# Down-projection: raw blocks in idle FFN slots by turns, second-half features stored split, gate weights split beside the last product

## The chip, the cores and the metric
The kernel runs on one core of a Trainium2 chip. Its engines are TensorE (PE, matmuls; PEld is its weight load), VectorE (DVE), ScalarE (ACT), GpSimd (POOL) and SyncE (SP), which here only issues DMAs. The metric is the time of one execution on the device in microseconds, median of several.

## The reference, cut to what matters
One decoder block in float32 on 1024 tokens of width 1024: two kinds of attention, an output projection, a gated MLP of width 2816, and a gated embedding added at the end. The change lies in the last two:

```python
h = rms_norm(x, g_pre_ffn[i])
u = causal_depthwise_conv(h @ w_up[i], conv_w[i], conv_b[i])
gate, val = jnp.split(u, 2, axis=-1)
f = (jax.nn.gelu(gate, approximate=True) * val) @ w_down[i]
x = x + rms_norm(f, g_post_ffn[i])
e = p[i] @ w_ple[i]
g = jax.nn.sigmoid(rms_norm(x, g_ple_gate[i]) @ w_ple_gate[i] + b_ple_gate[i])
x = x + rms_norm(g * e, g_post_ple[i])
```

## The kernel before
Every float32 operand of a matmul is split into a high part of type float32r (a cast on ACT, line 101) and the rest (a subtraction on DVE, or POOL, line 102); a product is high x high + low x high + high x low. `split` does this.

*Up-projection loop* (lines 1222 to 1250). 22 chunks of 128 features. For each chunk PE computes five products of 12 matmuls of a Strassen-like scheme. POOL and ACT prepare their weights, DVE adds partial sums into `u[0]` (gate) and `u[1]` (value), ACT writes the first tap of the convolution to PSUM (`y`), DVE adds two more, ACT applies gelu, DVE multiplies, and POOL stores the 128x1024 features to `f_dram[c]`. The loop's tiles live in the pool `up`: `p1`, `q0`, `q1` (128x512), `u0`, `u1`, `f` (128x1024), two slots each; `wr` with six slots for raw weights, `s` with four for sums.

*Down-projection* (from line 1305). The features of chunks 0 to 10 (first half) and 11 to 21 (second half), tokens 0 to 511 and 512 to 1023, and the two column halves of `w_down` make a 2x2x2 scheme with seven products instead of eight. Each product has 11 steps, one for each pair of chunks; each step (`down`) loads raw blocks, forms sums or differences on DVE, splits both operands, and issues 12 matmuls into four PSUM banks. The functions `p1` to `p7` say which blocks a product takes: product 7 takes a 128x1024 row of features (`both`, tag `u0`) and two weight blocks (tags `q0`, `q1`); product 2 takes second-half features of tokens 0 to 511 and a weight block (both `wr`), product 4 the second-half features of tokens 512 to 1023 and a weight block. The products run as 1 with 5, then 6 with 3, then 7 with 2, then the rest of 7, then 4. Raw blocks come on SP's queue. The split features go to `s`, the split weights to `wh`, `wl` of the pool `stage`.

*End.* `finish` adds the residual to each finished row of tokens and transposes its norm; its steps are spread by `fill` over the last steps of products 7 and 4 and the gate stage. In the gate stage each of eight token tiles takes 48 matmuls with 16 weight blocks of `w_ple_gate` (8 for each column half), which `gate_weights` loads and splits while the first tile runs. The gain and bias rows (`b_ple_gate`, `g_post_ple`) are loaded after product 4, in a pool `gp` that takes the place of `up`.

The program text gives dependences and priorities; a scheduler sets the order of instructions on each engine when the kernel is built, and each engine and queue then works through its list in that order.

Of the kernel before, what the change touches and what calls it, by code (L numbers as in the profile page):

```python
# [9 lines left out]
F32 = mybir.dt.float32  # L10
# [8 lines left out]
P = 128  # L19
# [34 lines left out]
def tile_hybrid_block(ctx: ExitStack, tc: tile.TileContext, a: dict, out: bass.AP):  # L54
# [1168 lines left out]
    for c in range(NCH):  # L1223
# [22 lines left out]
        y = [conv(v, c, u[v]) for v in range(2)]  # L1246
        f = up_tile("f", S, 2)
        act.activation(f, y[0], AF.Gelu_apprx_tanh)
        dve.tensor_tensor(f, f, y[1], ALU.mult)
        pool.dma_start(f_dram[c], f)  # L1250
    y_cm.__exit__(None, None, None)
# [65 lines left out]

    def loaded(src, tag):
        t = up_tile(tag, 512, WR if tag == "wr" else 2)
        sp.dma_start(t, src)  # L1320
        return t

    def f_blk(i, th, k, tag):
        return loaded(f_dram[i + NP * k][:, halves_of[th]], tag)

    def w_blk(i, k, dh, tag):
        c = i + NP * k
        return loaded(a["w_down"][c * P:(c + 1) * P, halves_of[dh]], tag)

    def both(src):  # L1330
        t = up_tile("u0", S, 2)
        sp.dma_start(t, src)
        return t[:, :H], t[:, H:]

    def sub(dst, x, y):
        dve.tensor_tensor(dst, x, y, ALU.subtract)
        return dst

    b22 = {}

    def p1(i):
        return f_blk(i, 0, 0, "wr"), w_blk(i, 0, 0, "wr")

    def p5(i):
        a21, a22 = f_blk(i, 1, 0, "q0"), f_blk(i, 1, 1, "q1")
        b11, b12 = both(a["w_down"][i * P:(i + 1) * P, :])
        dve.tensor_tensor(store[0][i], a21, a22, ALU.add)
        return store[0][i], sub(store[1][i], b12, b11)

    def p6(i):  # L1350
        a11, b22[i] = f_blk(i, 0, 0, "q0"), w_blk(i, 1, 1, "p1")
        return sub(store[0][i], store[0][i], a11), sub(store[1][i], b22[i], store[1][i])

    def p3(i):
        a12 = f_blk(i, 0, 1, "q1")
        return sub(a12, a12, store[0][i]), b22.pop(i)

    def p7(i):
        a11, a21 = both(f_dram[i])
        b12, b22_ = w_blk(i, 0, 1, "q0"), w_blk(i, 1, 1, "q1")  # L1360
        return sub(a11, a11, a21), sub(b22_, b22_, b12)

    def p2(i):
        return f_blk(i, 0, 1, "wr"), w_blk(i, 1, 0, "wr")

    def p4(i):
        a22, b21 = f_blk(i, 1, 1, "wr"), w_blk(i, 1, 0, "wr")
        return a22, sub(b21, b21, store[1][i])

    def down(product, i, banks, fresh):  # L1370

        fr, w = product(i)
        wh, wl = [stage.tile([P, 512], F32R, tag=x, name=nm(x), bufs=4) for x in ("wh", "wl")]
        fh, fl = [up.tile([P, 512], F32R, tag="s", name=nm("f"), bufs=4) for _ in "hl"]
        split(fh, fl, fr)
        split(wh, wl, w)
        for t in range(4):
            tk = slice(t * P, t * P + P)
            for n, (l_, r_) in enumerate(((fh, wh), (fl, wh), (fh, wl))):
                pe.matmul(banks[t], l_[:, tk], r_, start=fresh and i == 0 and n == 0,  # L1380
                          stop=i == NP - 1 and n == 2, skip_group_check=not fresh)
# [68 lines left out]
    wg = {}  # L1450

    def gate_weights():
        for dh in range(2):
            for k in range(NK):
                src = a["w_ple_gate"][k * P:(k + 1) * P, dh * 512:dh * 512 + 512]
                if len(wg) < 4:
                    wg[dh, k] = split_w(src, 512, g_ple_gate[:, k:k + 1])
                else:
                    w = stage.tile([P, 512], F32, tag="ws", name=nm("ws"), bufs=3)
                    sp.dma_start(w, src)  # L1460
                    wh = gp.tile([P, 512], F32R, tag=f"gh{dh}{k}", name=nm("gh"))
                    wl = gp.tile([P, 512], F32R, tag=f"gl{dh}{k}", name=nm("gl"))
                    split(wh, wl, w, g_ple_gate[:, k:k + 1])
                    wg[dh, k] = (wh, wl)
                yield

    gw = gate_weights()
    for t in range(NT):
# [7 lines left out]
        for n, (c0, c1) in enumerate(zip(cuts, cuts[1:])):  # L1476
# [4 lines left out]
            for k in range(NK):  # L1481
                if t == 0:
                    next(gw)
# [80 lines left out]
```

## Time and profile before
| | us |
|---|---|
| median of three runs (lowest, highest) | 1541.58 (1540.2, 1546.6) |
| profiled execution | 1545.03 |
| its span, first to last instruction | 1543.3 |
| PE busy | 1400.3 |
| DVE busy | 1083.3 |
| ACT busy | 827.1 |
| POOL busy | 532.4 |

Windows in the text are microseconds from the start of the span. The up loop fills PE from about 907 to 1185; the down-projection's matmuls run from 1179 to 1418, product 7 with 2 from about 1320 to 1383 and product 4 to 1418; the gate stage follows. Matmul ends are modelled and overlap, so a busy PE is not a PE at its peak: what it should take is better counted in matmuls. Idle time in a group's row stands behind the second bar, with what ended it.

### The profile page before, as it was taken

The numbers are of one execution on the slowest core, as the hardware profiler recorded it, in microseconds if no ns is written. First come the engines' busy times: TensorE is split into PE (matmuls) and PEld (weight loads), VectorE is DVE, ScalarE is ACT, GpSimd is POOL, SyncE is SP. The second block draws the span as 40 slices with busy tenths as digits, with TensorE's granted clock in tenths as the row PEclk, the third lists the DMA queues.
The fourth block names the chain that finished last, engine by engine and source line by source line (L and its number), as shares of the span: only waits on it lengthen the run. The fifth ranks groups of instructions, "written<-read, shape, count | busy, mean of one in ns | idle before, by whom it ended". The sixth has DMA issues, their size and how long they took to land. (4 is left out here: it accounts for less than half of the span.)

```text
span 1543.3 us, 20396 instructions
## 1 busy us (share of the span) xinstructions
PE 1400.3 (91%) x6684; PEld 1146.5 (74%) x6684; DVE 1083.3 (70%) x1916; ACT 827.1 (54%) x1565; POOL 532.4 (34%) x567
## 2 busy tenths in 40 slices
PE   5998998988799898989998899999999999888995
PEld 3977786876578786767786678888887778666874
DVE  4569467799677867853447657666778876678897
ACT  6356465677677756654534444444444454345642
POOL 7106300003134335122232199989881000000233
PEclk9999999999899999999999899999999999999998
DMA  6031310104445525255648534444446963755554
GB/s 202 23 103 41 109 35 7 55 30 154 120 127 157 154 79 173 100 156 179 217 142 285 188 117 164 164 164 154 153 155 211 367 193 98 224 185 184 170 194 149
DMA packets 128779, 226.99 MB, mean 147 GB/s; under 512 B 13456, under 2 KB 50224, under 8 KB 128672
## 3 DMA queue, kind: packets, MB, share of 16 engines
q1 hardware_dynamic: 111488, 166.57, 34.2%
q0 software_dynamic: 17184, 59.11, 10.4%
q8 instruction: 53, 0.87, 0.2%
q14 instruction: 54, 0.44, 0.1%
HBM read 170.31 MB, written 55.31 MB: 146 GB/s over the span
## 5 line engine op out<-in xcount | busy, mean ns | idle before, releaser
L102 DVE TENSOR_TENSOR tl<-tr,th 128x512 fp32r<-128x512 f32 x192 | 103.2, 550 | 40.8 <-ACT th L101 34.7
L1217 DVE SCALAR_TENSOR_TENSOR y<-u,c_conv_w,y 128x1023 f32<-128x1023 f32 (+1 forms) x88 | 112.5, 1284 | 25.9 <-ACT y L1215 24.8
L101 ACT CAST th<-tr 128x512 fp32r<-128x512 f32 x192 | 91.1, 485 | 56.7 <-PE tr L468 45.0
L102 POOL TENSOR_TENSOR ws<-s,ws 128x512 fp32r<-128x512 f32 x84 | 109.7, 1313 | 15.2 <-PE tr L921 7.8
L1380 PE MATMUL mm<-wh,f 128*128 128x512 f32 x352 | 112.0, 397 | 2.9 <-DVE f L102 2.7
L468 PE MATMUL tr<-ident,w 128*128 128x128 f32 x576 | 103.3, 287 | 11.8 <-DVE tl L102 6.2
L102 DVE TENSOR_TENSOR wl<-ws,wh 128x512 fp32r<-128x512 f32 x73 | 56.7, 785 | 70.7 <-ACT wh L101 41.9
L656 DVE TENSOR_TENSOR_SCAN kc<-kc,one_f 128x128 f32<-128x128 f32 (+3 forms) x64 | 88.0, 1382 | 13.0 <-ACT kc L653 12.9
L468 PEld LDWEIGHTS tr<-ident,w 128*128 128x128 f32 x576 | 74.5, 147 | 28.4 <-DVE tl L102 8.4
L483 PE MATMUL av<-tl,v 128*128 128x512 f32 x192 | 77.7, 406 | 18.0 <-DVE tl L102 17.2
L482 PE MATMUL av<-th,v 128*128 128x512 f32 x192 | 79.3, 413 | 12.3 <-ACT th L101 6.7
L1300 POOL DMA_DIRECT2D x_dram<-fd x8 | 4.4, 549 | 244.4 <-DVE fd L1299 244.4
L1380 PEld LDWEIGHTS mm<-wh,f 128*128 128x128 f32 x352 | 66.9, 190 | 20.1 <-DVE f L102 4.9
L1215 ACT ACTIVATE y<-u,c_conv_b,c_conv_w 128x1024 f32<-128x1024 f32 x44 | 53.2, 1210 | 51.3 <-DVE u L1243 22.0
L101 ACT CAST ws<-s 128x512 fp32r<-128x512 f32 x84 | 51.2, 613 | 53.4 <-PE tr L916 34.6
L101 ACT CAST wh<-ws 128x512 fp32r<-128x512 f32 x76 | 46.5, 621 | 61.7 <-DMA ws<-in_w_up 24.9
L752 POOL TENSOR_TENSOR t<-t,t 128x512 fp32r<-128x512 f32 x32 | 41.6, 1300 | 81.7 <-ACT t L751 36.5
L1380 PE MATMUL mm<-wl,f 128*128 128x512 f32 x176 | 69.6, 396 | 0.0
L124 PE MATMUL pj<-hTh,wh 128*128 128x512 f32 x160 | 65.5, 410 | 0.0
L125 PE MATMUL pj<-hTl,wh 128*128 128x512 f32 x160 | 64.1, 401 | 0.0
L126 PE MATMUL pj<-hTh,wl 128*128 128x512 f32 x160 | 64.1, 401 | 0.0
L1380 PE MATMUL tr<-wh,f 128*128 128x512 f32 x132 | 52.5, 402 | 11.3 <-DVE f L102 10.8
(517 smaller groups left out, 4465.6 us busy)
## 6 DMA issues: line engine op xcount, KB each, us to landing
wr<-in_w_up SPq DMA_DIRECT2D x84, 256.0 KB, 3.2
t<-o_dram SPq DMA_DIRECT2D x48, 256.0 KB, 3.1
ws<-in_w_up SPq DMA_DIRECT2D x47, 256.0 KB, 3.7
f_dram<-f POOLq DMA_DIRECT2D x22, 512.0 KB, 3.2
q<-f_dram SPq DMA_DIRECT2D x44, 256.0 KB, 4.5
wr<-f_dram SPq DMA_DIRECT2D x33, 256.0 KB, 4.2
wr<-in_w_down SPq DMA_DIRECT2D x33, 256.0 KB, 3.9
ws<-in_w_o SPq DMA_DIRECT2D x32, 256.0 KB, 3.2
```

The source lines that it names most:

```text
L101: act.copy(h, src)
L102: (pool if on_pool else dve).tensor_tensor(l, src, h, ALU.subtract)
L124: pe.matmul(ps, lh, rh, start=start, stop=False)
L125: pe.matmul(ps, lh, rl, start=False, stop=False)
L126: pe.matmul(ps, ll, rh, start=False, stop=stop)
L468: pe.transpose(tr[:, c:c + P], w[i][:, j * P:(j + 1) * P], ident)
L482: pe.matmul(av[:, lo:], v(j), th[:, lo:], start=j == 0, stop=False)
L483: pe.matmul(av[:, lo:], v(j), tl[:, lo:], start=False, stop=j == last)
L656: dve.tensor_tensor_scan(rev, rev, one_f[:, 0:1].to_broadcast([P, n]), 1.0, ALU.mult, ALU.mult)
L1215: act.activation(y, u, AF.Identity, bias=conv_b[:, ci:ci + 1], scale=conv_w[:, ci, 2:3])
L1217: dve.scalar_tensor_tensor(y[:, d:], u[:, :S - d], conv_w[:, ci, 2 - d:3 - d], y[:, d:], ALU.mult, ALU.add)
L1380: pe.matmul(banks[t], l_[:, tk], r_, start=fresh and i == 0 and n == 0, stop=i == NP - 1 and n == 2, skip_group_check=not fresh)
```

## The change
1. Each second-half chunk's product is written in place to PSUM (`y[1]`; the last one to `f`), split there to `fh`, `fl`, copied to `f` by ACT, and stored as `fs_dram` (high and low) as well as `f_dram`. The gelu is written in place to `u[0]`; `f` has one slot. All these stores are issued by ACT instead of POOL.
2. Products 2 and 4 load the second-half features already split (`f_split`), into `wr` slots (product 2), or into `s` slots and three pairs of slots of gate weights by turns (product 4). They are held until the matmuls have read them.
3. Raw blocks of products 5, 6, 3 and 7, of one step of product 1 and of the first four of product 2's weights take slots by turns: halves from `q0`, `q1`, `p1`, whole rows from `u0`, `u1`.
4. The loop's tiles except `wr` and `s` move to a pool `roles` that ends before product 4; the pool `gp` with bias, gain and gate weights starts there. Five gate weights are loaded and split beside product 4, three right after it, eight during the first tile.

```diff
+    up = ctx.enter_context(tc.tile_pool(name="up", bufs=1, side="right", reuse_waits="tile"))
+    roles_cm = tc.tile_pool(name="roles", bufs=1, side="right", reuse_waits="tile")
...
-        f = up_tile("f", S, 2)
-        act.activation(f, y[0], AF.Gelu_apprx_tanh)
-        dve.tensor_tensor(f, f, y[1], ALU.mult)
-        pool.dma_start(f_dram[c], f)
+        f = up_tile("f", S, 1)
+        act.activation(u[0], y[0], AF.Gelu_apprx_tanh)
+        g = y[1] if NCH // 2 <= c < NCH - 1 else f
+        dve.tensor_tensor(g, u[0], y[1], ALU.mult)
+        if c >= NCH // 2:
+            fs = [roles.tile([P, S], F32R, tag="f" + x, name=nm("f" + x)) for x in "hl"]
+            split(fs[0], fs[1], g)
+            if g is not f:
+                act.copy(f, g)
+            for x in range(2):
+                act.dma_start(fs_dram[c - NCH // 2][x], fs[x].bitcast(F32))
+        act.dma_start(f_dram[c], f)
...
+    raw_half = cycle([lambda x=x: up_tile(x, H, 2) for x in ("q0", "q1", "p1")])
+    raw_row = cycle([lambda x=x: up_tile(x, S, 2) for x in ("u0", "u1")])
+    def loaded(src, direct):
+        t = up_tile("wr", 512, WR) if direct else raw_half()
...
     def both(src):
-        t = up_tile("u0", S, 2)
+        t = raw_row()
...
+    def f_split(i, th):
+        fs = [late["fs"]() if th else up.tile([P, 512], F32R, tag="wr", name=nm("f"), bufs=WR)
+              for _ in "hl"]
+        for x in range(2):
+            sp.dma_start(fs[x].bitcast(F32), fs_dram[i][x][:, halves_of[th]])
+        return fs
...
     def p2(i):
-        return f_blk(i, 0, 1, "wr"), w_blk(i, 1, 0, "wr")
+        return f_split(i, 0), w_blk(i, 1, 0, i >= AHEAD_2)
     def p4(i):
-        a22, b21 = f_blk(i, 1, 1, "wr"), w_blk(i, 1, 0, "wr")
-        return a22, sub(b21, b21, store[1][i])
+        fs, b21 = f_split(i, 1), w_blk(i, 1, 0, True)
+        return fs, sub(b21, b21, store[1][i])
...
+    late["fs"] = cycle([lambda: up.tile([P, 512], F32R, tag="s", name=nm("f"), bufs=4)] * 4 +
+                       [lambda n=n, x=x: gate_tile(n, x) for n in (5, 6, 7) for x in "hl"])
...
     for i in range(NP):
         down(p4, i, group_z, True)
         fill.step(DOWN_RATE)
+        if i % 2 == 1:
+            gate_weight(i // 2)
...
+    for n in (5, 6, 7):
+        gate_weight(n)
```

Up to the gelu of the loop's first chunk, instructions stand as before on all engines. Three places show what moves after it. The names are tiles with buffer numbers; `ws` are the up-projection's split weights.

ACT, late in the second half of the up loop, before, from one chunk's gate tap to the next chunk's two taps (the value tap comes first):

```order
L1215 ACTIVATE y_2597_11146<-u_2583_11048,c_conv_b,c_conv_w 128x1024
L101 CAST ws_9090<-s_11240 128x512
L101 CAST ws_9090<-wr_11245 128x512
L1248 ACTIVATE f_11154<-y_2597_11146 128x1024
L101 CAST ws_9090<-s_11242 128x512
L101 CAST ws_9090<-s_11239 128x512
L101 CAST wh_11603<-wr_11601 128x512
L1215 ACTIVATE y_2616_11262<-u_2602_11161,c_conv_b,c_conv_w 128x1024
L101 CAST ws_9090<-s_11241 128x512
L1215 ACTIVATE y_2615_11258<-u_2601_11160,c_conv_b,c_conv_w 128x1024
```

ACT at the same place, now, from one chunk's gelu to the next chunk's two taps:

```order
L1252 ACTIVATE u_2595_11115<-y_2609_11213 128x1024
L103 CAST ws_9112<-s_11316 128x512
L103 CAST ws_9112<-s_11313 128x512
L103 CAST wh_11704<-wr_11702 128x512
L103 CAST fh_11224<-y_2610_11217 128x1024
L1262 DMA fs_dram6h<-fh_11224 128x1024
L103 CAST ws_9112<-s_11315 128x512
L1260 COPY f_11221<-y_2610_11217 128x1024
L1262 DMA fs_dram6l<-fl_11225 128x1024
L1219 ACTIVATE y_2629_11332<-u_2615_11234,c_conv_b,c_conv_w 128x1024
L1263 DMA f_dram_136<-f_11221 128x1024
L1219 ACTIVATE y_2630_11336<-u_2616_11235,c_conv_b,c_conv_w 128x1024
```

Between the gelu and the next chunk's value tap now stand the high part's cast, a copy of the product and two stores; the third store, of the copy, stands between the two taps.

SP, where products 7 and 2 run in turns, before (`u` and `q` are product 7's row and weights, `wr` product 2's):

```order
L1320 DMA q_3079_13274<-in_w_down 128x512
L1332 DMA u_3050_13164<-f_dram_126 128x1024
L1320 DMA q_3067_13226<-in_w_down 128x512
L1320 DMA wr_13371<-in_w_down 128x512
L1320 DMA wr_13394<-f_dram_131 128x512
L1320 DMA q_3086_13302<-in_w_down 128x512
L1332 DMA u_3065_13222<-f_dram_127 128x1024
L1320 DMA q_3080_13276<-in_w_down 128x512
```

SP there, now (`f<-fs_dram` and `wr` are product 2's):

```order
L1361 DMA f_13123<-fs_dram7h 128x512
L1338 DMA p_3077_13303<-in_w_down 128x512
L1338 DMA q_3064_13249<-in_w_down 128x512
L1350 DMA u_3076_13301<-f_dram_127 128x1024
L1361 DMA f_13124<-fs_dram7l 128x512
L1338 DMA wr_13127<-in_w_down 128x512
L1338 DMA q_3090_13353<-in_w_down 128x512
L1361 DMA f_13173<-fs_dram8h 128x512
L1338 DMA q_3078_13305<-in_w_down 128x512
L1350 DMA u_3089_13351<-f_dram_128 128x1024
L1361 DMA f_13174<-fs_dram8l 128x512
L1338 DMA wr_13177<-in_w_down 128x512
```

Each pair of steps now has two split feature blocks where one raw block was, and product 7's loads (`p`, `q`, `u`) stand further ahead of their use, among product 2's loads of other steps.

SP from the end of product 4's loads into the gate stage, before:

```order
L1320 DMA wr_13728<-in_w_down 128x512
L1320 DMA wr_13784<-f_dram_140 128x512
L1320 DMA wr_13786<-in_w_down 128x512
L112 DMA ws_13855<-in_w_ple_gate 128x512
L1273 DMA xl_13825<-e_dram 128x512
L1460 DMA ws_13864<-in_w_ple_gate 128x512
L1265 DMA b_ple_gate_13819<-in_b_ple_gate 128x1024
L1265 DMA g_post_ple_13821<-in_g_post_ple 128x1024
```

SP at the start of product 4's feature loads, now:

```order
L1338 DMA wr_13664<-in_w_down 128x512
L1338 DMA wr_13693<-in_w_down 128x512
L1278 DMA b_ple_gate_13452<-in_b_ple_gate 128x1024
L1278 DMA g_post_ple_13454<-in_g_post_ple 128x1024
L1361 DMA f_13456<-fs_dram0h 128x512
L1361 DMA f_13457<-fs_dram0l 128x512
L1361 DMA g_13530<-fs_dram2h 128x512
L1361 DMA g_13531<-fs_dram2l 128x512
L1361 DMA g_13586<-fs_dram3h 128x512
L1361 DMA f_13479<-fs_dram1h 128x512
L1361 DMA f_13480<-fs_dram1l 128x512
L1361 DMA g_13587<-fs_dram3l 128x512
```

The two broadcast rows moved from behind product 4's last load to a place ahead of its first feature loads, and these are now pairs of split halves in `f` and `g` slots; the gate weights follow further on, among its later loads.

More of the change, by code (lines that the diff above doesn't have):

```diff
@@ L72, in tile_hybrid_block @@
     f_dram = [dram.tile([P, S], F32, name=f"f_dram{c}") for c in range(NCH)]
+    fs_dram = [[dram.tile([P, S], F32, name=f"fs_dram{c}{x}") for x in "hl"]
+               for c in range(NCH // 2)]
     ident = const.tile([P, P], F32, name="ident")
@@ L1373, in down @@
         wh, wl = [stage.tile([P, 512], F32R, tag=x, name=nm(x), bufs=4) for x in ("wh", "wl")]
-        fh, fl = [up.tile([P, 512], F32R, tag="s", name=nm("f"), bufs=4) for _ in "hl"]
-        split(fh, fl, fr)
+        if isinstance(fr, list):
+            fh, fl = fr
+        else:
+            fh, fl = [up.tile([P, 512], F32R, tag="s", name=nm("f"), bufs=4) for _ in "hl"]
+            split(fh, fl, fr)
         split(wh, wl, w)
@@ L1436, in tile_hybrid_block, with gate_tile, gate_weight @@
     kept(group_y, 1, 0)
+    roles_cm.__exit__(None, None, None)
+    gp = ctx.enter_context(tc.tile_pool(name="gp", bufs=1, side="right", reuse_waits="tile"))
+    bg = bcast("b_ple_gate", gp)
+    gpp = bcast("g_post_ple", gp)
+    wg = {}
+    def gate_tile(n, x):
+        return gp.tile([P, 512], F32R, tag=f"g{x}{n}", name=nm("g"))
+    late["fs"] = cycle([lambda: up.tile([P, 512], F32R, tag="s", name=nm("f"), bufs=4)] * 4 +
+                       [lambda n=n, x=x: gate_tile(n, x) for n in (5, 6, 7) for x in "hl"])
+    def gate_weight(n):
+        dh, k = n // NK, n % NK
+        w = load_w(a["w_ple_gate"][k * P:(k + 1) * P, dh * 512:dh * 512 + 512])
+        if n < NK:
+            wg[dh, k] = [gate_tile(n, x) for x in "hl"]
+        else:
+            p_, tags, bufs = ((stage, ("wh", "wl"), (4, 4)) if n < NK + 4 else
+                              (up, ("s", "wr"), (4, WR)))
+            wg[dh, k] = [p_.tile([P, 512], F32R, tag=x, name=nm("g"), bufs=b)
+                         for x, b in zip(tags, bufs)]
+        split(*wg[dh, k], w, g_ple_gate[:, k:k + 1])
     for i in range(NP):
@@ L1443, in tile_hybrid_block @@
     finish(1)
-    up_cm.__exit__(None, None, None)
-    gp = ctx.enter_context(tc.tile_pool(name="gp", bufs=1, side="right", reuse_waits="tile"))
-    bg = bcast("b_ple_gate", gp)
-    gpp = bcast("g_post_ple", gp)
-    wg = {}
-    def gate_weights():
[L1453 to L1465, printed above, removed]
+    for n in (5, 6, 7):
+        gate_weight(n)
+    def gate_weights():
+        for n in range(NK, 2 * NK):
+            gate_weight(n)
+            yield
     gw = gate_weights()
@@ L1482, in tile_hybrid_block @@
                 if t == 0:
-                    next(gw)
+                    next(gw, None)
                 wh, wl = wg[dh, k]
```

26 lines of the change are left out of this document (12 added, 14 removed).

## The prediction, made before the change was run
> **What bounds the kernel now.** I read the engine summary first, then busy time by stretch, then who waited for whom inside the stretches that lose time, then single groups for durations.
>
> ```profile
> PE 1400.3 (91%) x6684; PEld 1146.5 (74%) x6684; DVE 1083.3 (70%) x1916; ACT 827.1 (54%) x1565; POOL 532.4 (34%) x567
> ```
>
> TensorE (PE) is the bound on average, so only time in which it stands still can be won. The stretches (width, then busy time and count of PE, PEld, DVE, ACT, POOL; granted clock; DMA share, GB/s) say where that is:
>
> ```profile
> 907.30:1185.30 278.00, 277.33 (x1224) 229.27 (x1223) 192.48 (x210) 128.67 (x162) 231.59 (x194) 1.00 0.48 158
> 1185.30:1200.20 14.90, 12.11 (x50) 8.83 (x49) 13.90 (x19) 7.40 (x11) 2.15 (x4) 1.00 0.94 344
> 1200.00:1220.00 20.00, 20.00 (x89) 16.42 (x88) 16.57 (x27) 8.64 (x16) 0.54 (x1) 1.00 1.04 395
> 1320.00:1383.00 63.00, 54.90 (x231) 42.46 (x230) 39.40 (x69) 22.92 (x40) 0.00 (x0) 1.00 0.63 208
> 1383.00:1418.40 35.40, 33.54 (x144) 27.11 (x144) 30.08 (x74) 20.91 (x37) 1.61 (x3) 0.95 0.52 171
> 1418.40:1432.00 13.60, 9.82 (x35) 7.23 (x34) 11.72 (x31) 7.97 (x13) 1.07 (x2) 0.75 0.71 221
> 1432.00:1518.00 86.00, 79.49 (x367) 64.11 (x366) 77.44 (x254) 45.09 (x85) 26.76 (x31) 1.00 0.54 180
> ...
> L1291 PE MATMUL tr<-ident,xs 128*128 128x128 f32 x64 | 9.3, 294 | 2.6 <-ACT xs L1286 2.6
> ```
>
> The first is the up-projection loop: 1224 matmuls in 278.0 us, 0.227 us each, so a chunk of 60 takes 13.6 us and PE never stops. At 0.227 (0.145 for each of the small transposes: the last row's 9.3 us for 64) the other stretches should take: end of the loop 50 x 0.227 = 11.4, lost 3.5; products 7 and 2 (1320 to 1383) 231 x 0.227 = 52.4, lost 10.6; product 4 (136 matmuls, 8 transposes) 32.0, lost 3.4; head of the gate stage (27 and 8) 7.3, lost 6.3, part of it the clock at 0.75; the rest of the gate stage (319 and 48) 79.4, lost 6.6. About 30 us in all. The waits of these stretches (who waited for whom: us, times, longest):
>
> ```profile
> PE tr L1380 <- DVE f L102: 8.1, 8, 1.5
> DVE u L1336 <- DMA u<-f_dram: 18.5, 7, 4.1
> SPq L1320 <- DVE q L1336: 22.9, 6, 5.1
> SPq L1332 <- DVE f L102: 9.1, 8, 4.0
> ...
> PE mm L1380 <- DVE f L102: 1.9, 1, 1.9
> PE mm L124 <- ACT gh L104: 2.9, 1, 2.9
> PE tr L1291 <- ACT xs L1286: 2.4, 2, 1.5
> PE mm L124 <- ACT bh L101: 1.7, 1, 1.7
> ```
>
> The first four are products 7 and 2. PE waits for a split, VectorE (DVE) behind it for a landing, and SyncE's queue (SP) waits to issue that load until DVE frees one of two slots. DMA is busy 0.63 of that time: latency through too few slots, not bandwidth. The last ones: gate weights that come late, then rows that DVE, busy 77.4 of 86 us, hands over late.
>
> **The change, part by part.** Durations (landing times of loads in products 7 and 2; three issues on SP, start and length; groups with mean ns behind the busy time):
>
> ```profile
> u<-f_dram SPq DMA_DIRECT2D x8, 512.0 KB, 4.3
> wr<-f_dram SPq DMA_DIRECT2D x10, 256.0 KB, 4.6
> wr<-in_w_down SPq DMA_DIRECT2D x10, 256.0 KB, 4.6
> ...
> 1341.09 0.33 SPq L1320 DMA_DIRECT2D q<-in_w_down  x1
> 1341.69 0.33 SPq L1332 DMA_DIRECT2D u<-f_dram  x1
> 1342.30 0.33 SPq L1320 DMA_DIRECT2D q<-in_w_down  x1
> ...
> L1215 ACT ACTIVATE y<-u,c_conv_b,c_conv_w 128x1024 f32<-128x1024 f32 x42 | 50.7, 1210 | 48.7 <-issue 21.8 <-DVE u L1243 20.3 <-DVE u L1245 6.7
> L1248 ACT ACTIVATE f<-y 128x1024 f32<-128x1024 f32 x22 | 22.6, 1028 | 21.8 <-DVE y L1217 19.1 <-issue 2.0 <-ACT ws L101 0.8
> L1249 DVE TENSOR_TENSOR f<-f,y 128x1024 f32<-128x1024 f32 x22 | 26.9, 1221 | 11.3 <-ACT f L1248 11.3
> L1243 DVE TENSOR_TENSOR u<-p,tr 128x512 f32<-128x512 f32 x21 | 14.4, 687 | 42.5 <-PE tr L921 42.5
> L1250 POOL DMA_DIRECT2D f_dram<-f x21 | 11.8, 561 | 29.8 <-DVE f L1249 27.8 <-ACT wh L101 2.0
> L102 DVE TENSOR_TENSOR f<-wr,f 128x512 fp32r<-128x512 f32 x20 | 13.7, 687 | 1.4 <-ACT f L101 1.2
> L105 DVE SCALAR_TENSOR_TENSOR gl<-ws,c_g_ple_gate,gh 128x512 fp32r<-128x512 f32 x12 | 8.8, 747 | 1.4 <-ACT gh L104 1.4
> ```
>
> *Up loop.* In 11 chunks come one cast of 128x1024 on ScalarE (ACT; nearest row L1248, 1.03), one DVE subtraction (nearest L1249, 1.22), in 10 of them a copy on ACT (1.03 again), and 22 stores; the 22 old stores leave GpSimd (0.56 each, 12.3 us of POOL off the path) for ACT. An issue on ACT has no row; SP's is 0.33 and holds its queue 0.60. Per chunk of 13.6 us DVE goes from 192.48/278 x 13.6 = 9.4 to 10.6, ACT from 6.3 to 6.3 + 2.06 + 3 x 0.33 to 0.60 = 9.4 to 10.2, POOL from 11.3 to 10.8. None reaches 13.6; PE covers them. As a chain, the product must be cast (1.03), then subtracted (1.22), then copied (1.03), the low half's store issued (0.6), and only then ACT does the next chunk's first y (1.21). DVE is left idle 3 us a chunk to take that up, and before it stood 2.0 (42.5 for 21) a chunk at L1243 waiting for PE. Taken: 0.7 us lost; ends from -1 (POOL issues no stores) to +20 (a rival).
>
> *End of the loop.* DVE is busy 13.90 of 14.9 us and gets two more subtractions (2.4); DMA, at 0.94, gets 1 MB more per chunk. Against that the order brings product 1's third split forward. Taken: 1.5 lost; ends 0 and 4.
>
> *Products 7 and 2.* Product 7 has four rows instead of two and six halves turning over three names; its waits for landings (18.5 us) go, since a row is now issued several pairs ahead. Product 2 gets its f ready split: 11 casts and 11 subtractions (0.69) fewer, but a third block. Three of six `wr` slots per product, and now held until the matmuls are done, leave two products of depth. Its last load can be issued when the product before the last ends, 36 matmuls or 8.2 us ahead. Ahead of it on SP stand five others at 0.60 (3.0), landing takes 4.6, the cast 0.6: 8.2. Late next, then, is product 2's own weight block, by a little: taken 0.3 us per pair over eight pairs and 0.5 at the seam, 3.0 left of 10.6. Gain 7.6; ends 3.6 and 10.6.
>
> *Product 4.* f again comes split (11 subtractions fewer), b21 as before, and five gate splits (0.75 on DVE, as much on ACT) stand between. Its first two f pairs need `s` slots that product 7 holds until its last two matmul groups end: lead 12 x 0.227 = 2.7, landing 4.6 + 0.6 for the second block, stall 2.5. On SP these loads stand behind the two broadcast rows, which wait for product 7's slots to come free. Volume: 22 f blocks, 5 weights not yet there, 5 gate blocks, 4 for the two broadcast rows, 8 for rows in and out: 44 of 0.262 MB = 11.5 MB, at the 395 GB/s of the fullest row 29.2 us, beside 32.0 of PE. That is 0.9 of the DMA; taken 1.9 more of stalls. 4.4 lost for 3.4: -1.0; ends +2 and -6.
> [...]
>
> *Gate stage.* Eight of sixteen weights are split before the first tile needs them: head 6.3 to 1.0 (three splits and the last additions are still in front), gain 5.3; ends 2 and 6.3. The rest waits for rows from DVE, which from product 4 on does 11 x 0.69 = 7.6 us less; five gate splits only move within that stretch. Taken 1.5 of 6.6; ends 0 and 6. The last tile's tail is untouched.
>
> Sum: -0.7 - 1.5 + 7.6 - 1.0 + 5.3 + 1.5 = 11.2 us. The profiled execution took 1545.03 (span 1543.3 and 1.73 around it), so 1533.8 in its terms; it lay 3.45 above the median, which gives 1541.58 - 11.2 = **1530.4**.
>
> **Rivals.**
> *DMA eats it.* The split f doubles its bytes; in a pair of products 7 and 2 seven blocks (1.84 MB) take 4.65 us of 5.45. If bursts queue, 7.0 of the 10.6 stay and product 4 loses 5 more than before: 3.6 - 5 + 5.3 + 1.5 - 2.2 = 3.2, 1538.4. For it: share 1.04 at 1200 to 1220 and landings of 4.6 at 0.63. Against: PE did not stall in that fullest stretch.
> [...]
> *The loop's second half becomes the bound (slower).* ACT runs in order, and its casts of weights stand waiting for PE:
>
> ```profile
> ACT ws L101 <- PE tr L916: 64.2, 37, 4.8
> ```
>
> That is 1.7 us each time. If such a cast stands in front of the new one, mult to cast to subtraction to the next y slips by about 2.0 in each of ten chunks: 20 lost and 0.7 not counted, 1541.58 - 11.9 + 20 = 1549.7. It cancels the gain from 1.2 a chunk on. Against: in the order above two of these casts stand ahead of the new one, and the products that they wait for should be done by then.
> *The end of the kernel is DVE's.* If rows come as much earlier as DVE has less to do, the gate stage's rest loses 2 instead of 6.6, products 7 and 2 only 0.5, product 4 as before, the up loop and its end nothing: 10.1 + 5.3 + 4.6 = 20, 1521.6. For it: DVE busy 0.9 there. Against: each row also waits for its own loads and sums.
>
> **Numbers.** Half a per cent (7.7 us) is about what a measurement of this kernel can tell from no change. The forecast (1526 to 1536) has 0.50, DMA 0.23, the slower loop 0.12, the gain of 20 0.15. Faster than 1533.9: 0.40 + 0.15 + 0.03 = 0.58; slower than 1549.3: 0.09; between: 0.33. Range 1520 to 1544: it leaves out the slower loop's upper part and the best end.
>
> **What would show it.** In the profile after: PE still full in the up loop at 13.6 us a chunk (else the second rival); waits for u from f_dram gone from products 7 and 2, with PE's wait there at 2 to 3 us and DMA share above 0.8; one gap of 2 to 3 us at product 4's first f; no wait for gate weights in the first tile; the first row's transposes ahead of product 4's end. DMA at 1.0 through product 4 with PE in gaps would be the first rival. Wrong altogether if SP, in order, stands on a slot of product 2 while product 7's loads queue behind it.

## The result and the profile after
The changed kernel takes 1536.55 us (median of 19 runs) against 1542.76 for the kernel before (19 runs too). The ratio is 0.9948 (95% interval 0.9936 to 0.9961): 8.0 us of 1542.76 by the ratio, 6.2 by the medians. The prediction was 1530.4 in 1520 to 1544, a gain of 11.2. The time lies inside the range and the direction is right; the gain is half to three quarters of the forecast. One of the changed kernel's 19 runs took 3446 us, in a slow state; it counts in the median, not in the ratio.

The profiled execution took 1540.11 us, 4.92 less than that of before. The engine summary of the changed kernel:

```profile
PE 1400.1 (91%) x6684; PEld 1149.4 (75%) x6684; DVE 1080.4 (70%) x1905; ACT 833.1 (54%) x1564; POOL 523.6 (34%) x545
```

PE's work is the same; what changed is where PE stands still. Busy time by stretch of the changed kernel (width, then busy time and count of PE, PEld, DVE, ACT, POOL; granted clock; DMA share, GB/s), with the stretch boundaries at its own products: up loop, its end, products 7 and 2, product 4, and the gate stage's head:

```profile
907.30:1185.30 278.00, 277.32 (x1223) 229.26 (x1223) 202.40 (x218) 144.38 (x179) 222.92 (x174) 1.00 0.56 190
1187.70:1215.00 27.30, 19.64 (x69) 14.36 (x68) 22.03 (x30) 12.88 (x18) 1.66 (x3) 0.87 0.99 374
1319.90:1387.90 68.00, 63.38 (x266) 50.45 (x265) 39.92 (x68) 20.95 (x37) 0.00 (x0) 0.97 0.74 240
1387.90:1426.00 38.10, 33.79 (x149) 27.51 (x148) 31.51 (x89) 21.13 (x35) 2.68 (x5) 0.96 0.85 304
1426.00:1442.00 16.00, 16.00 (x74) 13.12 (x73) 14.03 (x35) 8.79 (x14) 1.49 (x1) 1.00 0.46 150
```

The up loop is as full as before, 1223 matmuls in 278.0 us. At its end only 69 matmuls run in 27.3 us; the same stretch of the kernel before:

```profile
1187.70:1215.00 27.30, 24.51 (x104) 18.99 (x103) 24.65 (x37) 12.43 (x20) 2.15 (x4) 1.00 1.01 380
```

That is 35 matmuls, 8 us, lost to the change. In return the gate stage's head has no wait at all: 74 matmuls in 16 us at full clock.

To compare versions, the whole is cut at matmuls and not at times: a pair of products is always 264 matmuls, and a stretch ends where its last matmul starts, so a stall ahead of the next product counts with that product. Cut so, products 1 and 5 took 69.4 us in the profiled execution of before and 77.5 in the changed one; products 6 and 3 62.0 and 62.8; 7 and 2 72.3 and 67.9; product 4 34.8 and 38.1; from its last matmul to the end 125.2 and 112.3. So -8.1, -0.8, +4.4, -3.3, +12.9; -0.2 before the first matmul; together 4.9.

Who waited for whom at the loop's end, in products 7 and 2, and in product 4 of the changed kernel (us, times, longest):

```profile
PE tr L1408 <- DVE f L104: 5.9, 3, 3.6
DVE st L1354 <- DMA u<-in_w_down: 2.4, 1, 2.4
PE tr L1408 <- ACT f L103: 1.6, 1, 1.6
...
ACT wh L103 <- DMA wr<-in_w_down: 24.2, 6, 5.9
DVE u L1354 <- DMA u<-f_dram: 9.1, 6, 3.1
PE mm L1408 <- ACT wh L103: 3.1, 2, 1.8
...
PE mm L1408 <- DMA f<-fs_dram0h: 4.3, 1, 4.3
```

At the loop's end DVE waits for a raw row and PE behind it for splits. In products 7 and 2 PE's longest waits are now for product 2's own weight block. In product 4 it is one gap, for the first feature block.

### The profile page after: what moved, and what is told of

Its sections match the earlier page's. It is cut to its first block, busy times and chain, and to the rows that moved or that the text cites. A ratio compares the mean times of both kernels' runs of the same rounds, so it can differ in the third digit from the quotient of the medians.

```text
span 1538.3 us, 20415 instructions
## 1 busy us (share of the span) xinstructions
PE 1400.1 (91%) x6684; PEld 1149.4 (75%) x6684; DVE 1080.4 (70%) x1905; ACT 833.1 (54%) x1564; POOL 523.6 (34%) x545
## 5 line engine op out<-in xcount | busy, mean ns | idle before, releaser
L1408 PE MATMUL mm<-wh,f 128*128 128x512 f32 x304 | 96.1, 406 | 7.4 <-DMA f<-fs_dram0h 4.3
L658 DVE TENSOR_TENSOR_SCAN kc<-kc,one_f 128x128 f32<-128x128 f32 (+3 forms) x64 | 89.4, 1403 | 12.7 <-ACT kc L655 12.6
L1408 PEld LDWEIGHTS mm<-wh,f 128*128 128x128 f32 x304 | 58.7, 194 | 22.3 <-DMA f<-fs_dram0h 4.7
L485 PEld LDWEIGHTS av<-tl,v 128*128 128x128 f32 x192 | 38.3, 200 | 34.2 <-DVE tl L104 32.0
L916 PE MATMUL mm<-bh,wh 128*128 128x512 f32 x136 | 55.6, 409 | 6.1 <-ACT wh L103 4.3
```

The source lines that it names most:

```text
L485: pe.matmul(av[:, lo:], v(j), tl[:, lo:], start=False, stop=j == last)
L658: dve.tensor_tensor_scan(rev, rev, one_f[:, 0:1].to_broadcast([P, n]), 1.0, ALU.mult, ALU.mult)
L916: pe.matmul(ps, w[0][:, ks], b[0][:, k], start=start and k == 0, stop=False, skip_group_check=not start)
```

## The experiments
Each version below was timed and profiled. In the table, "lost" is a stretch's length without 0.2245 us for each 512-column matmul in it (about the closest spacing that the traces show, 0.224, so some tenths more is lost than by the prediction's 0.227; half of it for 256 columns, whose closest spacing in the changed kernel is 0.113) and 0.059 for a small transpose (those of line 494 in the kernel before start 0.057 to 0.063 us apart). The transposes of these stretches lie 0.108 us apart at their closest, and eight of them take 0.79 us up to the next matmul, so the columns for product 4 and the gate stage hold 0.04 us too much for each: 0.3 for product 4 with 8 of them, 0.6 with 16. A stall that the text gives by itself is counted in the same way, from matmul start to matmul start; the profile's own figure, which lets the modelled end of the matmul before it pass first, is some 0.2 lower. "Tail" runs from the last matmul's start to the end; the sum runs from the first down-projection matmul to the end. What lies ahead of that matmul differs between executions without cause in the edits (the up loop's last 1200 matmuls took 273.0 us in every one, but began anywhere from 902.4 to 913.0), so profiles are compared by the sum, and times by the ratio to before.

| version | 1, 5 lost | 7, 2 lost | 4 lost | gate lost | tail | sum | ratio (interval) |
|---|---|---|---|---|---|---|---|
| before | 5.0 | 13.1 | 4.7 | 20.0 | 15.5 | 363.8 | 1 |
| the change | 13.1 | 8.7 | 7.6 | 8.4 | 14.8 | 358.6 | 0.9948 (0.9936, 0.9961) |
| late_rows | 10.9 | 7.3 | 7.4 | 11.1 | 14.6 | 356.7 | 0.9957 (0.9937, 0.9977) |
| whole_last | 9.2 | 5.6 | 8.6 | 8.9 | 15.7 | 352.8 | 0.9944 (0.9923, 0.9966) |
| xl_late | 10.5 | 8.8 | 8.6 | 8.5 | 11.9 | 352.2 | 0.9943 (0.9919, 0.9968) |
| slots_only | 5.5 | 6.4 | 2.5 | 18.7 | 12.0 | 350.5 | 0.9912 (0.9878, 0.9945) |
| slots_again | 5.8 | 8.0 | 2.4 | 19.3 | 12.0 | 353.2 | 0.9920 (0.9897, 0.9943) |
| slots_gate | 6.4 | 7.0 | 3.8 | 19.4 | 15.6 | 356.9 | 0.9981 (0.9963, 0.9999) |
| inplace | 9.4 | 6.7 | 2.5 | 17.4 | 13.4 | 355.5 | 0.9967 (0.9949, 0.9986) |
| p4_raw | 10.7 | 5.8 | 8.4 | 15.3 | 10.6 | 356.6 | 0.9968 (0.9946, 0.9990) |
| split_fixed | 9.4 | 14.9 | 5.5 | 12.1 | 14.8 | 360.5 | 1.0003 (0.9981, 1.0024) |
| gate_after | 11.4 | 8.6 | 7.5 | 8.1 | 14.8 | 356.2 | 0.9954 (0.9938, 0.9970) |
| gelu_fl | 11.6 | 7.0 | 6.4 | 8.4 | 14.8 | 352.1 | 0.9933 (0.9913, 0.9953) |
| half_split | 13.8 | 7.2 | 9.0 | 13.1 | 16.4 | 365.0 | 1.0004 (0.9984, 1.0024) |

The same kernel twice (slots_only, slots_again) differs by up to 1.6 in a column and 2.7 in the sum; less than that means nothing here (products 1 and 5, which late_rows and gate_after leave alone, differ by 2.2 between them and the changed kernel). Expectations of the first four runs counted losses in fixed windows of time, so their figures differ from the table's by some tenths to some us.

My theory after the result: the slots gain in products 7 and 2, the early gate weights gain at the head of the gate stage, and the split features cost at the loop's end (more stores at a DMA share of 0.99) and at product 4's start (loads that cannot be issued early). Its rivals: DVE, not DMA, makes the loss at the loop's end, and DVE, not the weights, makes the gain in the gate stage.

**slots_only: one part of the change alone.**

```diff
 # the kernel before, and:
+    raw_half = cycle([lambda x=x: up_tile(x, H, 2) for x in ("q0", "q1", "p1")])
+    raw_row = cycle([lambda x=x: up_tile(x, S, 2) for x in ("u0", "u1")])
     def loaded(src, tag):
-        t = up_tile(tag, 512, WR if tag == "wr" else 2)
+        t = up_tile("wr", 512, WR) if tag == "wr" else raw_half()
     def both(src):
-        t = up_tile("u0", S, 2)
+        t = raw_row()
```

> The kernel before with one part of the change: raw halves take q0, q1, p1 by turns and raw rows u0, u1. No split features, no earlier gate weights. Theory (products 7 and 2 gained by the deeper slots of product 7): PE's loss at 1320 to 1383 falls from 10.4 to about 6, that of products 6 and 3 from 2.3 to about 0, the rest stays; 5 to 6 us faster than before. Rival (it was DVE, rid of product 2's subtractions): the loss there stays at 8 or more and the time within 2 us of before.

> The raw slots by turns alone, a second time, for a closer figure of the fastest version so far (ratio 0.9912, interval 0.9878 to 0.9945, from 5 runs). If that holds: 0.990 to 0.993. If it was luck of few runs: 0.994 to 0.996, as the changed kernel.

Products 7 and 2 lose 6.4 (8.0 the second time) for 13.1, and the whole is 13.6 and 12.3 us faster by the ratios, more than the full change. Waits in its products 7 and 2 (slots_again):

```profile
DVE u L1339 <- DMA u<-f_dram: 14.5, 6, 3.5
PE tr L1383 <- DVE f L102: 4.4, 4, 1.2
```

DVE still waits 14.5 us for landings, before 18.5, but it now does so further ahead of PE, which waits 4.4 for 8.1. Of the gain in the sum (13.3 us, by the second timing's profile 10.6) 6.7 and 5.1 lie in products 7 and 2. Another 3.5 are the tail and 2.2 product 4, where no edit was made: in the last tile DVE's list stands in another order, and a stall of 2.0 us in product 4 of the kernel before is gone, with the 3.4 us behind it in which the granted clock was 0.50 (half clock, below). About half of the gain is thus shown to be the slots'; the rest I put down to the order that the scheduler wrote, which no run isolates.

**split_fixed: the change without that part.**

```diff
 # the changed kernel, and:
-        t = up_tile("wr", 512, WR) if direct else raw_half()
+        t = up_tile(tag, 512, WR if tag == "wr" else 2)   # each block in the name it had before
-        t = raw_row()
+        t = up_tile("u0", S, 2)
```

> The changed kernel without its slots by turns: raw blocks in the one name each that they had before. Split features and early gate weights stay. Theory (products 7 and 2 gain by the slots and not by ready features): they lose 12 us or more, as before (13.1), where the changed kernel lost 8.7, and products 1 and 5 as in the changed kernel, 11 to 13; 4 us slower than the changed kernel. Rival (ready features relieve DVE there): they lose 9 or less and the time is the changed kernel's.

Products 7 and 2 lose 14.9, as before the change or more, and the gain is gone (1.0003). Ready features by themselves bring nothing there; the slots make the gain of products 7 and 2, shown from both sides. Products 1 and 5 lost 9.4, where 11 to 13 was expected.

**late_rows: what stands ahead of product 4's first features.**

```diff
 # the changed kernel, and:
-    bg = bcast("b_ple_gate", gp)
-    gpp = bcast("g_post_ple", gp)
     for i in range(NP):
         down(p4, i, group_z, True)
         fill.step(DOWN_RATE)
+        if i == 6:
+            bg = bcast("b_ple_gate", gp)
+            gpp = bcast("g_post_ple", gp)
```

> The changed kernel with the two broadcast rows loaded beside product 4's sixth step instead of ahead of its first features. In the changed kernel's profile PE lost 8.5 us at 1383 to 1418 (4.2 before), most of it in two gaps, 1.7 and 4.5, the second ended by the landing of product 4's first feature block, issued at 1385.5 right behind the rows and landed at 1392.5. Theory (the rows' 1 MB stands ahead in the DMA queue): about 2.6 us at 395 GB/s go from that landing, the loss falls to 5.5 to 6.5 and the kernel is 2 to 3 us faster than the changed one. Rival (the slots set the start: product 7's last steps give them back at 1385): the landing stays within 1 us, the time the same; and if the rows then come late for the gate stage's first additions, 1 to 2 us slower.

The first block is still issued 2.4 us ahead of the matmul that needs it, with the pair of another step ahead of it now; it lands 5.7 us behind its issue instead of 7.0, and the gap shrank from 4.5 to 3.2. But product 4 still lost 7.4 and the time is the changed kernel's. The clock took back what the gap gave. In the first 6.04 us behind it (changed kernel, then late_rows; columns as above) the granted clock was 0.72 and 0.50, and 19 and 14 matmuls ran, 5 x 0.2245 = 1.1 us:

```profile
1392.59:1398.63 6.04, 6.04 (x19) 4.82 (x20) 3.34 (x9) 1.24 (x3) 0.00 (x0) 0.72 1.04 383
```

```profile
1390.06:1396.10 6.04, 6.04 (x14) 4.78 (x15) 2.60 (x7) 2.06 (x4) 0.00 (x0) 0.50 1.03 395
```

SP's list in the changed kernel at that place:

```profile
1384.98 0.43 SPq L1278 DMA_DIRECT2D g_post_ple<-in_g_post_ple  x1
1385.52 0.36 SPq L1361 DMA_DIRECT2D f<-fs_dram0h  x1
1385.98 0.38 SPq L1361 DMA_DIRECT2D f<-fs_dram0l  x1
```

PE reaches product 4 at 1387.9. The rows ahead cost some 1.3 us; the rest is that these loads are issued so close to the end of product 7.

**p4_raw: product 4 loads raw again.**

```diff
 # the changed kernel, and:
     def p4(i):
-        fs, b21 = f_split(i, 1), w_blk(i, 1, 0, True)
-        return fs, sub(b21, b21, store[1][i])
+        a22, b21 = f_blk(i, 1, 1, True), w_blk(i, 1, 0, True)
+        return a22, sub(b21, b21, store[1][i])
```

> The changed kernel, but product 4 loads its second-half features raw and splits them as before; product 2 still loads them split. Theory (blocks held until the matmuls are done keep product 4's first loads from being issued early): no gap of 3 us or more at product 4's first matmuls, the loss of product 4 falls from 7.6 to 3 to 4, the time by 3 to 5 from the changed kernel's. Rival (DVE, with 11 more subtractions of 0.69 beside product 4, hands the rows over later): product 4 gains as much, but the gate stage loses 3 to 5 more than 8.4 and the time is the same.

Neither came as expected. The one gap is gone, and five others stand in its place (four of 0.8 to 1.0 on DVE, one of 3.1 on a weight's cast): product 4 loses 8.4. The gate stage loses 15.3 for 8.4, which is the rival's part. Split features beside product 4 thus buy time on DVE.

**whole_last and xl_late: stores, or DVE, at the loop's end.**

```diff
 # whole_last: the changed kernel, and (LAST = 2):
-        if c >= NCH // 2:
+        if NCH // 2 <= c < NCH - LAST:
     def f_split(i, th):
+        if i >= NP - LAST:
+            return f_blk(i, th, 1, True)
```

> The changed kernel, but the last two chunks are neither split in the up loop nor stored split: products 2 and 4 load and split them as before. In the changed kernel's profile PE lost 13.5 us at 1187 to 1260 where before it lost 4.5. Theory (2 MB more of stores at the loop's end push the first down-projection loads back: one issued at 1188.8 landed at 1199.2): the loss falls to 5 to 6, two steps each of products 2 and 4 pay 0.7 us of DVE again, and the kernel is 5 to 8 us faster than the changed one. Rival (DVE's order and its two 1.22 us subtractions make the loss): it falls by 2 to 3 us only, with the landings unchanged.

```diff
 # xl_late: the changed kernel, and for the first four rows, in xl_tile:
+        if after is not None:
+            pool.tensor_tensor(t[:, :512], after, after, ALU.add)
         queue.dma_start(t, src)
```

> The changed kernel, with the loads of the first four residual rows (three of them are issued by POOL at 1188.3 to 1189.5, 512 KB each) held back until product 1's sums are in the rows, by a POOL addition of 128x512 that writes into the tile first. Nothing of the split features changes. Theory (DMA at the loop's end is full): 1.5 MB less there is 3.9 us at 395 GB/s; the loads of product 5's blocks land 2 to 4 us earlier, the loss at 1187 to 1260 falls from 13.5 to 8 to 10, 3 to 5 us faster than the changed kernel. Rival (DVE's order): nothing moves by more than 1 us.

In the windows of these expectations (73 us from 7.3 us behind the first down-projection matmul, with 0.227 us for each matmul) the changed kernel lost 13.5, late_rows and gate_after, which leave this place alone, 11.5 and 11.9, xl_late 9.4 and whole_last 8.3. Against those three whole_last gains some 3 to 5, between the two expectations. By the times neither version is told apart from the changed kernel (0.9944 and 0.9943 for 0.9948). xl_late's figure is within the theory's 8 to 10, but only 2.1 to 2.5 of it is beyond what the place does by itself, though the loads did land earlier: one issued 9.1 us behind the first matmul took 6.3 us instead of 10.4. DVE's list in xl_late, behind the last landing that it waits for:

```profile
1201.53 0.69 DVE L1374 TENSOR_TENSOR st<-p,q 128x512 f32<-128x512 f32 x1 [0.90 <-DMA q<-f_dram]
1202.14 0.68 DVE L104 TENSOR_TENSOR f<-q,f 128x512 fp32r<-128x512 f32 x1
1202.74 2.47 DVE L1221 SCALAR_TENSOR_TENSOR y<-u,c_conv_w,y 128x1022 f32<-128x1022 f32 x2
...
1208.13 1.28 DVE L1221 SCALAR_TENSOR_TENSOR y<-u,c_conv_w,y 128x1022 f32<-128x1022 f32 x1
1209.32 0.68 DVE L104 TENSOR_TENSOR f<-wr,f 128x512 fp32r<-128x512 f32 x1
```

From 1201.5 until then it is never idle, and PE's last stall (3.4 us at 1210.06) ends with the split of 1209.32. So with these loads early DVE's own list is the bound of that stall. The residual rows' traffic is worth some 2 us of the 6 to 8 lost here. The split features' stores were still there, and the three issued 9.3 to 12.6 us behind the first matmul took 6.9 to 7.9 us to land, so they are not cleared; for the larger part the rival is the likelier, but not shown.

**inplace and gelu_fl: the gelu in u0.**

```diff
 # inplace: slots_only, and:
-        f = up_tile("f", S, 2)
-        act.activation(f, y[0], AF.Gelu_apprx_tanh)
-        dve.tensor_tensor(f, f, y[1], ALU.mult)
+        f = up_tile("f", S, 1)
+        act.activation(u[0], y[0], AF.Gelu_apprx_tanh)
+        dve.tensor_tensor(f, u[0], y[1], ALU.mult)
```

> The raw slots alone, and the up loop's product as the change has it but not its splitting: the gelu written in place to the first half's row u0, and one slot for f in place of two; no more stores, no more work on DVE. Theory (u0's slots come free later, so the first raw rows of product 5 are issued later): the loss of products 1 and 5 rises from 5.5 to 8 to 10 us, as where the last two chunks weren't split (9.2), and the time by 3 to 4. Rival (the split stores and subtractions alone make the loss at the loop's end): it stays at 5 to 6.

In products 1 and 5 it came as the theory had it: 9.4 lost, 3.9 us of the gain gone (3.6 by the second timing of the slots alone), with no more work and no more bytes. By the ratios it is 7 to 8.5 us slower than the slots alone, twice what was expected; the tail shows 1.4 of that. The second raw row is issued 6.3 us behind the first down-projection matmul (1185.51 in the first row) instead of 3.9, since the u0 slot is held until the product is formed. The next load (`p`) goes out 6.9 us behind that matmul in both versions, but now 0.6 us behind the row instead of 2.9, and it lands in 5.7 us instead of 3.8. DVE waits for that landing with the split that PE needs behind it. SP's list and DVE's list of inplace, the same two of slots_only, and PE's wait in inplace:

```profile
1185.51 0.33 SPq L1335 DMA_DIRECT2D u<-in_w_down  x1
1186.11 0.32 SPq L1323 DMA_DIRECT2D p<-f_dram  x1
...
1191.92 0.69 DVE L1350 TENSOR_TENSOR st<-q,p 128x512 f32<-128x512 f32 x1 [1.19 <-DMA p<-f_dram]
1192.53 2.47 DVE L1217 SCALAR_TENSOR_TENSOR y<-u,c_conv_w,y 128x1023 f32<-128x1023 f32 x2
1194.91 1.28 DVE L102 TENSOR_TENSOR f<-wr,f 128x512 fp32r<-128x512 f32 x2
```

```profile
1180.27 0.33 SPq L1335 DMA_DIRECT2D u<-in_w_down  x1
1183.19 0.32 SPq L1323 DMA_DIRECT2D p<-f_dram  x1
...
1187.74 0.69 DVE L1350 TENSOR_TENSOR st<-q,p 128x512 f32<-128x512 f32 x1
1188.35 1.28 DVE L1217 SCALAR_TENSOR_TENSOR y<-u,c_conv_w,y 128x1023 f32<-128x1023 f32 x1
1189.54 0.69 DVE L102 TENSOR_TENSOR f<-wr,f 128x512 fp32r<-128x512 f32 x1
```

```profile
PE tr L1383 <- DVE f L102: 4.2, 1, 4.2
```

Behind the first matmul the split starts at 15.7 us here and at 13.2 in slots_only. Of the difference 1.2 us is the wait for the landing and 1.2 one more tap of the convolution that stands ahead of the split in DVE's list. PE's stall grows by about as much, from 1.8 us to 4.2. A landing late by 1.2 us thus cost PE 1.2 us here and no multiple of it; the rest of the stall is what the list has ahead of the split. And the stall is not the whole loss: for 5.95 us behind it the granted clock is 0.50, and 14 matmuls run there. Of the 9.4 us lost, stalls are 5.0 and matmuls at half clock 2.9. In slots_only these two are 3.5 and 0, in slots_again 2.6 and 1.6, in the changed kernel 8.2 and 3.0, before 3.3 and 0.

```diff
 # gelu_fl: the changed kernel, and:
-        act.activation(u[0], y[0], AF.Gelu_apprx_tanh)
-        dve.tensor_tensor(g, u[0], y[1], ALU.mult)
+        e = fs[1].bitcast(F32) if c >= NCH // 2 else f   # fs is made before this
+        act.activation(e, y[0], AF.Gelu_apprx_tanh)
+        dve.tensor_tensor(g, e, y[1], ALU.mult)
```

> The changed kernel with the gelu written to the tile of the low part instead of in place to u0 (to f in the chunks that aren't split), so that u0 is free again as soon as the taps have read it. Work, stores and loads are the same. Theory (the loss at the loop's end comes mostly from raw rows that wait for u0): products 1 and 5 lose 7 to 9 instead of 11 to 13, 3 to 5 us faster than the changed kernel. Rival (stores and subtractions): they still lose 10.5 or more.

Here the theory fell: 11.6, although the second raw row went out 5.3 us behind the first matmul, in the changed kernel 8.6. By its median it is the fastest version with split features (0.9933), but not for that reason. Two things can each make the loss at the loop's end: raw rows that wait for u0 (inplace), and the splitting with its stores (gelu_fl). Only where both are away does it lose 5 to 6.4. Whether the subtractions or the stores make the second stays open: xl_late points to DVE's list, but in gelu_fl DVE also stood 2.1 us on a raw row that took 12.8 us to land.

**slots_gate and gate_after: what the early gate weights are worth.** slots_gate is slots_only with the pools `roles` and `gp`, `gate_tile` and `gate_weight` of the change, whose calls beside product 4 stay, and no split features.

> The kernel before with two parts of the change, the raw slots by turns and the gate weights split beside product 4; no split features. From the first down-projection matmul to the end the slots alone took 350.5 us (before 363.8, the whole change 358.6); in its gate stage PE still lost 18.7 us, with the whole change 8.4. Theory (the early gate weights make that gain, and split features only cost): gate stage 8 to 10 lost, product 4 about 4 for 2.5, the rest as with the slots alone: 340 to 343 us, a time of 1520 to 1523. Rival (the gate stage gained because split features relieve DVE beside product 4): it loses 14 or more, the time is 1526 to 1530.

```diff
 # gate_after: the changed kernel, and:
-        if i % 2 == 1:
-            gate_weight(i // 2)
...
-    for n in (5, 6, 7):
+    for n in range(NK):
         gate_weight(n)
```

> The changed kernel, with none of the gate weights beside product 4: all are loaded and split behind it. In the first 16 us behind product 4's last matmul PE lost 7.2 us before, 0.3 with the whole change, 8.5 with the early gate weights but no split features (the second row's transposes stood 18 us behind there, 2.2 us ahead in the changed kernel). Theory (the head needs both, weights and rows): rows early and weights late, the head loses 4 to 7 again, on the gate weights, and the time is 4 to 6 above the changed kernel's. Rival (only the early rows made the head's gain): it loses under 2 and the time is the changed kernel's.

With slots_gate that part of the theory fell, and its time, 1538.6, is above both expectations. Eight gate weights are split beside product 4 and the gate stage loses 19.4, as before, 8.5 of it in the first 16 us. The wait only changes its name. PE's waits in those 16 us, of slots_again (weights late), then of slots_gate (weights early):

```profile
PE mm L124 <- ACT gh L104: 3.5, 1, 3.5
```

```profile
PE mm L124 <- ACT bh L101: 3.1, 1, 3.1
PE mm L126 <- DVE bh L102: 1.4, 1, 1.4
```

`gh` is a gate weight, `bh` the normed row: in slots_gate the first row comes late. What DVE did beside product 4, in slots_gate, then in the changed kernel (groups: busy, mean ns):

```profile
L102 DVE TENSOR_TENSOR f<-wr,f 128x512 fp32r<-128x512 f32 x11 | 7.4, 683 | 0.0
L105 DVE SCALAR_TENSOR_TENSOR g<-ws,c_g_ple_gate,g 128x512 fp32r<-128x512 f32 x8 | 6.0, 746 | 1.0 <-ACT g L104 1.0
L1300 DVE SCALAR_TENSOR_TENSOR fd<-fd,rn,g_post_ffn 128x1024 f32<-128x1024 f32 x1 | 1.3, 1280 | 0.0
```

```profile
L107 DVE SCALAR_TENSOR_TENSOR g<-ws,c_g_ple_gate,g 128x512 fp32r<-128x512 f32 x9 | 6.6, 745 | 0.5 <-ACT g L106 0.4
L1311 DVE SCALAR_TENSOR_TENSOR fd<-fd,rn,g_post_ffn 128x1024 f32<-128x1024 f32 x3 | 3.9, 1283 | 0.1
```

Eleven feature splits and eight gate splits left room for one row; nine gate splits alone left room for three, in a stretch that is 4.6 us longer. In the changed kernel the first row's transposes stand at 1413.52, 12.5 us ahead of product 4's last matmul, and the second row's at 1423.78, 2.2 ahead; in slots_gate at 1415.62 and 1433.45, 0.2 and 18 us behind it:

```profile
1413.52 1.04 PE L1304 MATMUL tr<-ident,xs 128*128 128x128 f32 x8
1423.78 1.04 PE L1304 MATMUL tr<-ident,xs 128*128 128x128 f32 x8
```

```profile
1415.62 1.05 PE L1293 MATMUL tr<-ident,xs 128*128 128x128 f32 x8
1433.45 1.03 PE L1293 MATMUL tr<-ident,xs 128*128 128x128 f32 x8
```

A rival is that the longer product 4 makes the room, and p4_raw bears on it: eleven raw features and nine gate splits beside a product 4 of 38.5 us, its first row's transposes 7.1 us ahead, and 65 matmuls in the gate stage's first 16 us, where slots_gate has 41 and the changed kernel 74. But there the loss has only moved. From the start of product 4 to the kernel's last matmul, so without the tail, slots_gate took 143.0 us, p4_raw 143.4, the slots alone 140.9 and 141.5, and the whole change 135.7. So the early weights pay where the split features have cleared DVE beside product 4; without them they brought nothing, and the kernel is slower with them than with the slots alone (0.9981 for 0.9912 and 0.9920). gate_after tells nothing on this: the scheduler put all sixteen gate splits within 0.5 us of where they stand in the changed kernel, so it seems to be the pools and not the calls' place in the text that let them go early. Rows early with weights late was therefore not measured.

**half_split: the sum of what seemed to pay.** Only the second 512 columns of a chunk are split and stored, for product 4; product 2 is raw, `f` has two slots and is written as before.

```diff
 # the changed kernel, and:
+            fs = [roles.tile([P, H], F32R, tag="f" + x, name=nm("f" + x)) for x in "hl"]
+            split(fs[0], fs[1], f[:, H:])
...
-        return f_split(i, 0), w_blk(i, 1, 0, i >= AHEAD_2)
+        return f_blk(i, 0, 1, True), w_blk(i, 1, 0, True)
```

> The changed kernel, with only what product 4 reads stored split: the second 512 columns of a chunk; product 2 loads raw and splits as before. The tiles of half the width leave room for two slots of f, and the gelu and the product are written to f as before, its store is POOL's again. If all that the runs so far showed adds up: products 1 and 5 lose about 6.5 (slots alone 5.5), 7 and 2 6.5, product 4 7 to 8, the gate stage 8 to 10: from the first down-projection matmul to the end 345 to 349 us where the slots alone took 350.5 and the whole change 358.6, a time of 1524 to 1529. Rival (product 2's ready features are needed for early rows too): the gate stage loses 13 or more, and the time is 1530 to 1533.

Neither: 365.0, a ratio of 1.0004. Products 1 and 5 lose 13.8; ACT stood 7.6 us on the landing of a raw row and PE 4.7 behind it. The gate stage loses 13.1, the rival's figure, but not for the rival's reason: the first two rows' transposes stand 12.5 and 2.2 us ahead of product 4's last matmul, as in the changed kernel, and the longest stall, 3.8 us, is on a later row. Parts don't add up here. That each edit has the scheduler write another order for DVE, ACT and SP is my explanation, but no run shows it; the cause stays open.

## Why the prediction was right, and where it was not
By its steps, forecast and the two profiled executions:
- *Up loop* -0.7, measured 0.0: its last 1200 matmuls take 273.0 us in both. DVE went from 192.5 to 202.4 us of 278, ACT from 128.7 to 144.4. The rival by which ACT's order slows the loop is out.
- *End of the loop* -1.5 (0 to 4 lost), measured -8.1, and about -6 in two more runs that leave this place alone. This step failed. Its terms (DVE's 2.4 us, the extra megabyte) were there, but three things were missing: that the in-place gelu holds u0 and sends raw rows out later, which by itself cost 3.6 to 3.9 us in inplace; that DVE's list has taps and other splits ahead of the one that PE needs; and the clock, for of the 8.1 us stalls are 4.9 and matmuls at a granted clock of 0.50 3.0. How much of what inplace doesn't show is the subtractions' and how much the stores' stays open.
- *Products 7 and 2* +7.6, measured +4.4 (and -0.8 in 6 and 3). That product 2's own weight block would be late next was right: two waits of 3.1 us in all, where 3.0 was left over. But the stretch lost 8.7: a stall of 1.7 us on a split at product 7's end and 1.6 by 3.4 us at half clock behind the second of those waits were not in the sum. That the waits for u from f_dram would go was wrong: 9.1 us of them stay, ahead of PE's need. The cause was named in two halves, slots and ready features; split_fixed and slots_only show the slots alone.
- *Product 4* -1.0, measured -3.3. The place and kind of the stall were right. It was 4.5 us instead of 2.5, since the first block took 7.0 us to land and not 4.6, and 3.4 us at half clock behind it cost another 1.6, as much as the clock cost in product 4 before. The 1.7 us stall just ahead counts with product 7 here.
- *Gate stage* +6.8 for head and rest, measured +12.9 to the end. The head lost 0.3 for 7.2. That gain was put down to the weights alone, and slots_gate shows that by themselves they give none; the rows have to be there too, and they come early with DVE's 7.6 us less, to which I gave 1.5.

That the sum came near is luck in part: the two undersized losses and the oversized slots (some 13 us) were half paid by the undersized gain at the gate stage (6 us). The rival *DMA eats it* gave nearly the measured time, and in part for its reason: the two weight blocks that PE waited for in products 7 and 2 took 6.0 and 5.7 us to land, and product 4's first block 7.0, where 4.6 was taken. But the losses that remain in products 7 and 2 came at a DMA share of 0.74, more than a third of them from the stall on a split and the clock, and the largest loss, at the loop's end, is 1.5 in this rival's sum as in the forecast. The 395 GB/s by which the forecast divided product 4's volume is matched by the rows below, 391 to 419.

The fastest version is the slots by turns alone, at 1530.2 and 1530.7 us in its two timings; the interval of gelu_fl's ratio overlaps both of its own.

## What to carry to other kernels
Deeper slots for loads that are waited for late are cheap, and by themselves they were worth more here than the whole change; a part that moves work to an engine's idle time has to be counted against that engine's list in the stage where it lands, not against its mean. When two parts share an engine, try each by itself and both: here the early weights lost without the features' relief. And where a scheduler writes the order, a few us in places that no edit touches (3.5 in the last tile) come and go with any edit, so one run of one part proves little below that. Count matmuls behind a stall as well as the stall: half clock behind it was worth 3.0 us in products 1 and 5 of the changed kernel, as much as the difference between two versions, and nothing in slots_only.

## What the runs showed that I had not expected
A stall here cost more than its length. Around the gap of 3.8 us at 1205.99 the changed kernel's clock and matmul counts are

```profile
1200.00:1205.90 5.90, 1.18 (x4) 0.67 (x4) 5.90 (x9) 1.63 (x3) 0.00 (x0) 0.94 1.03 413
1206.00:1210.00 4.00, 4.00 (x10) 3.13 (x11) 3.49 (x5) 1.61 (x3) 0.00 (x0) 0.50 1.06 409
1210.00:1214.00 4.00, 4.00 (x15) 3.23 (x14) 3.01 (x6) 1.14 (x4) 0.00 (x0) 0.75 1.02 391
1214.00:1218.00 4.00, 4.00 (x19) 3.30 (x18) 2.75 (x5) 1.48 (x4) 0.00 (x0) 1.00 1.03 416
```

25 matmuls in 8 us where 35 fit at 0.227: 2.3 us more, at a granted clock of 0.50 and then 0.75 (up to 1211.7 the matmuls start 0.43 us apart), with PE shown as fully busy. A stall did not always bring this. Both profiles of the slots alone (slots_only, then slots_again) have the same wait of 1.8 us at the same place (it ends at 1190.28 and 1189.34); from 1.1 us behind it the clock was 1.00 in one and 0.50 in the other:

```profile
1191.40:1194.80 3.40, 2.83 (x13) 2.01 (x12) 3.40 (x5) 1.14 (x2) 0.00 (x0) 1.00 1.03 419
```

```profile
1190.45:1193.85 3.40, 3.40 (x10) 2.66 (x9) 3.40 (x5) 1.14 (x2) 0.00 (x0) 0.50 1.03 411
```

So in this case the length of the stall alone does not tell whether the clock falls. The prediction put part of one stretch's loss down to a clock of 0.75, but counted its new stalls without it. And a DMA issue on ACT took 0.33 to 0.36 us for the split stores of the changed kernel, close to the 0.33 of SP's rows in the prediction:

```profile
1175.75 0.33 ACTq L1262 DMA_DIRECT2D fs_dram8h<-fh  x1
```
